# Sixteen moved tiles 96 bytes longer: where the operands of a two-layer encoder's large projections begin in memory

## The chip, the cores and the metric

The kernel runs on one core of a Trainium2 chip. The metric is the device time of one execution in microseconds (us). TensorE's clock has two levels here, 1.2 and 2.4 GHz; the trace gives the granted share of the full one.

## The reference

A trunk of two layers on 512 tokens of 1024 channels, all in float32. Each layer normalizes x, scales and shifts it by vectors that come from a condition c, projects it, mixes along the tokens, projects back, adds the result to x by a gate, and then does the same with a gated feed-forward block with a short convolution (ConvFFN, inner width 2816).

```
h = rmsnorm(x) * (1 + scale) + shift
layer 0: p = h @ ab_w_in;  y = [HGRN2 recurrence, 4 heads | RWKV-7 mixing, 8 heads](p)
layer 1: p = h @ cd_w_in;  y = [2-D Fourier mix, 4 groups | Conformer convolution](p)
x = x + gate * (y @ w_out)
u, v = split(rmsnorm(x)*(1 + scale) + shift) @ w_up)
x = x + gate * ((silu(dwconv3(u)) * v) @ w_down)
...
return rmsnorm(x) * final_g
```

## The kernel before

Activations lie with channels on the 128 partitions and the 512 tokens along the row, so x is eight tiles of 128 x 512. A projection to 128 output channels is a sum over eight input blocks in one PSUM bank. To reach float32 accuracy, each operand is split into a rounded high half and the rest (`split`, `modulate`, `load_w`), and each block costs three matmuls in `mm3` (lines 138, 139, 140): high weights by high x, high weights by low x, low weights by high x. The activations are the moved operand (512 columns); a slice of 128 x 128 weights is loaded for each matmul.

The tiles with tag "h" are that moved operand for the large input projections, the ConvFFN's up projection and the layers' output projections: 16 buffers in `hpool`, eight high and eight low halves. The same 16 buffers also serve as eight accumulators of layer 0's early output projection (`early_out`, line 867) and as the eight output tiles (line 1082). The down projection of the ConvFFN moves tiles of another pool, tag "g" (22 buffers, line 345 on); the Fourier part moves four tables of 2 x 258 columns, "tab" and "tabl" (lines 941 to 972), against weights "vh" and "vl" that come from the activations.

Memory is laid out in the order in which pools are opened, each tile rounded up to a multiple of 32 bytes a partition. First comes a scratch of 16384 bytes, then small constants, then the weight tiles (`raw` of 4096 bytes, `whi` and `wlo` of 2048), then the sixteen h tiles of 2048 bytes, then the pools of the stages. A tile "pad" of 224 bytes among the constants (line 110) makes the weight tiles begin at a multiple of 512, so the weight slices (512 bytes each), the h tiles and the g tiles all begin at multiples of 512 bytes in each partition. In the pool of layer 1, four padded inputs of 2168 bytes and the tables of 2064 bytes lie ahead of vh and vl: the four tables begin at 0, 32, 64 and 96 modulo 512 (the second half of each 8 bytes further), vh and vl at 128. The temporaries "ht" and "ot" of layer 0 begin at 416 and 288 modulo 512, the tiles "ss", "sq" and "x" at multiples of 512. The memory is full to 229152 bytes a partition.

The order of instructions on each engine comes from the framework's planner, which simulates times from the shapes of the operations and from priorities that the kernel gives (`PLAN`, `URGENT`). All transfers are issued by SyncE (SP). Weight blocks are loaded into one of three `raw` buffers, split by ScalarE (line 132) and VectorE (line 133), and then used by eight groups of three matmuls.

Of the kernel before, what the change touches and what calls it, by code (L numbers as in the profile page):

```python
# [9 lines left out]
F32 = mybir.dt.float32  # L10
F32R = mybir.dt.float32r
# [5 lines left out]
P = 128  # L17
T = 512
# [49 lines left out]
def encoder(ctx: ExitStack, tc: tile.TileContext, A, out, dbg=None):  # L68
    nc = tc.nc
    uid = [0]  # L70

    def mk(pool, shape, tag, dtype=F32, bufs=None):
        uid[0] += 1
        kw = {} if bufs is None else {"bufs": bufs}
        return pool.tile(shape, dtype, tag=tag, name=f"{tag}_{uid[0]}", **kw)
# [9 lines left out]
    hpool = ctx.enter_context(tc.tile_pool(name="hpool", bufs=16))  # L85
# [7 lines left out]
    def gps(shape=(P, T)):  # L93
        turn[0] += 1
        return mps(shape, gtags[0][turn[0] % len(gtags[0])])

    def mps(shape=(P, T), tag="m"):
        return mk(psum, list(shape), tag, bufs=banks[tag])

# [20 lines left out]
    def load_w(src, nk, pool=None, bufs=None):  # L120
        if pool is None:
            pool, bufs = spools[0]
            spools.append(spools.pop(0))
        raw = mk(wpool, [P, 8, P], "raw", bufs=3)
        nc.sync.dma_start(raw[:, :nk, :], src)
        w = []
        for k0 in range(0, nk, 4):
            n = min(4, nk - k0)
            hi = mk(pool, [P, 4, P], "whi", F32R, bufs=bufs)
            lo = mk(pool, [P, 4, P], "wlo", F32R, bufs=bufs)  # L130
            with tc.high_priority(URGENT):
                act.copy(hi[:, :n, :], raw[:, k0:k0 + n, :])  # L132
                dve.tensor_tensor(lo[:, :n, :], raw[:, k0:k0 + n, :], hi[:, :n, :].bitcast(F32), op=ALU.subtract)  # L133
            w += [(hi[:, i, :], lo[:, i, :]) for i in range(n)]
        return w
# [6 lines left out]
    def gemm(ps, w, xs, nk):  # L142
        for k in range(nk):
            mm3(ps, w[k][0], w[k][1], xs[k][0], xs[k][1], k == 0, k == nk - 1)

    def split(src):
        hi = mk(hpool, [P, T], "h", F32R)
        lo = mk(hpool, [P, T], "h", F32R)
        act.copy(hi, src)
        dve.tensor_tensor(lo, src, hi.bitcast(F32), op=ALU.subtract)  # L150
        return hi, lo

    def modulate(t, x, rs, scale, shift):

        hi = mk(hpool, [P, T], "h", F32R)
        lo = mk(hpool, [P, T], "h", F32R)
        dve.scalar_tensor_tensor(t, x, scale, rs, op0=ALU.mult, op1=ALU.mult)
        act.activation(hi, t, AF.Identity, bias=shift)  # L158
        dve.scalar_tensor_tensor(lo, t, shift, hi.bitcast(F32), op0=ALU.add, op1=ALU.subtract)  # L159
        return hi, lo  # L160
# [40 lines left out]
    def adaln(l, s, ch, tag):  # L201

        pa = mps([P, 256], tag)
        for k in range(KB):
            raw = mk(wpool, [P, 8, P], "raw", bufs=3)
            nc.sync.dma_start(raw, A["ada1"][ADA1.index((l, s, ch)), k])
            v = raw.rearrange("p g (q i) -> p q g i", q=4)
            for q in range(4):
                pe.matmul(pa[32 * q:32 * q + 32, :], sc32[:, k, :], v[:, q],
                          start=(k == 0), stop=(k == KB - 1), skip_group_check=True)  # L210
        mt = mk(const, [P, 8, 32], "mt", bufs=1)
        dve.transpose(mt.rearrange("p g i -> p (g i)"), pa)
        dve.tensor_copy(mods[l, s][0][:, ch * 8:ch * 8 + 8], mt[:, :, 0])
        finish(l, s, ch)
# [5 lines left out]
    def sc_row(pool):  # L220

        row = mk(pool, [P, D], "row")
        for i in range(2):
            ps = mps()
            for j in range(4):
                pe.matmul(ps[:, j * P:j * P + P], sc[:, 4 * i + j:4 * i + j + 1].broadcast_to([P, P]), ident,
                          start=True, stop=True)
            act.copy(row[:, i * T:i * T + T], ps)
        return row
# [31 lines left out]
    def modulated(x, mod, gsc, pool):  # L261
        rs = rstd_of(x, pool)
        hs = []
        for b in range(KB):
            t = mk(pool, [P, T], "nt", bufs=3)
            hs.append(modulate(t, x[b], rs, gsc[:, b:b + 1], mod[:, b:b + 1]))
        return hs
# [7 lines left out]
    def start_in(pool, pool2):  # L275
# [22 lines left out]
        for b in range(KB):  # L298
            raw = mk(pool, [P, 2, D], "ada", bufs=ADB)
            nc.sync.dma_start(raw, A["ada0"][b])  # L300
            if b < len(ps):
                ws[FIRST[b]] = load_w(A["ab_in"][FIRST[b]], KB, pool2, 2 * len(ps) - 2)
            with tc.high_priority(2 * URGENT):
                for i in range(2):
                    dot(raw[:, i], row, mod[:, b + 8 * i:b + 8 * i + 1])
                dve.tensor_tensor(mod[:, b:b + 9:8], mod[:, b:b + 9:8], col("ada_b", b, 9)[:, ::8], op=ALU.add)
                dve.scalar_tensor_tensor(gsc[:, b:b + 1], mod[:, 8 + b:9 + b], 1.0, col("norm_g", b), op0=ALU.add, op1=ALU.mult)
                t = mk(pool, [P, T], "nt", bufs=3)
                hs.append(modulate(t, x[b], rs, gsc[:, b:b + 1], mod[:, b:b + 1]))
# [51 lines left out]
    def layer0(ys):  # L361
# [4 lines left out]
        def lap():  # L366
            return mk(kp, [P, T], "la", bufs=4)
# [308 lines left out]
        def rwkv_post(q):  # L676
# [33 lines left out]
            if p == 3:  # L710
                late[1] = split(y)
            else:
                nc.sync.dma_start(ys[4 + p], y)
# [38 lines left out]
        def hgrn(h):  # L752
# [94 lines left out]
            if h == 3:  # L847
                late[0] = split(y)
            else:
                nc.sync.dma_start(ys[h], y)  # L850
            say(f"ya{h}", y)

        def early_out(acc, i):

            yy = []
            for k in EARLY[i]:
                y = lap()
                nc.sync.dma_start(y, ys[k])
                yy.append(split(y))
            for o in range(KB):  # L860
                if o == 4:
                    yield
                w = load_w(A["ab_out1"][i, o], len(yy))
                ps = gps()
                gemm(ps, w, yy, len(yy))
                if len(acc) == o:
                    acc.append(mk(hpool, [P, T], "h"))
                    before = lap()
                    nc.sync.dma_start(before, A["xT"][o])
                else:  # L870
                    before = acc[o]
                dve.scalar_tensor_tensor(acc[o], ps, mods[0, 0][0][:, 16 + o:17 + o], before, op0=ALU.mult, op1=ALU.add)
# [4 lines left out]
        def gate(_):  # L877
# [9 lines left out]
            "chain1": lambda p: rwkv_chain(pairs[p], units[p, 1], 1),  # L887
            "post": lambda p: rwkv_post(pairs[p]), "proj": hgrn_proj, "hgrn": hgrn, "gate": gate,
            "ada": lambda p: adaln(*ADA1[p], "g"), "out": lambda p: early_out(early, p)}
        begun, left = {}, {}  # L890

# [187 lines left out]
    for b in range(KB):  # L1079
        act.activation(x[b], x[b], AF.Copy, scale=col("final_g", b))  # L1080
    for b in range(KB):
        o = mk(hpool, [P, T], "h")
        (pl if b in (2, 5) else dve).tensor_tensor(o, x[b], rs, op=ALU.mult)
        nc.sync.dma_start(out[b], o)

# [60 lines left out]
```

## Time and profile before

| | |
|---|---|
| median of 3 runs | 1535.62 us (1531.64 to 1535.84) |
| the profiled execution | 1533.86 us, span 1532.0 us |
| TensorE busy | 1423.4 us (93%), 8114 matmuls |
| VectorE busy | 1036.5 us (68%) |
| ScalarE busy | 684.7 us (45%) |
| GpSimd busy | 160.3 us (10%) |
| mean granted TensorE clock | 0.944 |

The span runs from the first to the last instruction of the profiled execution. Layer 0 up to its output projection takes the first 615 us, its ConvFFN ends at about 985 us, layer 1's mixing at about 1150 us, and the second ConvFFN at about 1520 us; the final normalization and the stores follow. Busy matmuls overlap in the trace, since they are pipelined; the distance between their starts is what counts.

### The profile page before, as it was taken

What the parts mean: (1) busy time and instruction counts of PE and PEld (TensorE: products, weight loads), DVE (VectorE), ACT (ScalarE), POOL (GpSimd) and SP (SyncE); (2) the same over time, 40 slices, a digit from 0 to 9 for tenths busy, and PEclk for the clock granted to TensorE, in tenths of its full rate; (3) what the DMA queues carried; (4) which work ended last, traced back from release to release, by engine and by line L of the source; (5) the groups of instructions that cost most, each with busy time, mean ns of one, the idle gap of its engine ahead of it and who ended that gap; (6) DMA issues with size and microseconds to landing.
All of it is one profiled execution on the core that took longest, in us unless ns stands there. A gap on an engine that the chain in (4) does not pass through costs nothing.

```text
span 1532.0 us, 21743 instructions
## 1 busy us (share of the span) xinstructions
PE 1423.4 (93%) x8114; PEld 1108.1 (72%) x8114; DVE 1036.5 (68%) x2056; ACT 684.7 (45%) x1192; POOL 160.3 (10%) x224
## 2 busy tenths in 40 slices
PE   5988879998999998899999999898888999999996
PEld 3765666765767766688888888676756888888885
DVE  7678977697686857766566775679967653544544
ACT  4455454645544624543243243476555332332344
POOL 1030211101100000000000000069700000000000
PEclk7998888998997999999999999999899999999998
DMA  9211212332341444244544872221122332223222
GB/s 374 83 62 53 48 54 73 100 99 72 86 151 38 130 152 140 102 149 160 187 143 141 278 261 89 83 92 60 49 76 99 121 96 98 97 86 107 97 86 79
DMA packets 76282, 174.26 MB, mean 114 GB/s; under 512 B 28176, under 2 KB 33168, under 8 KB 75152
## 3 DMA queue, kind: packets, MB, share of 16 engines
q1 hardware_dynamic: 76176, 172.87, 34.3%
q8 instruction: 64, 1.05, 0.3%
q14 instruction: 42, 0.34, 0.1%
HBM read 166.02 MB, written 6.82 MB: 113 GB/s over the span
## 4 chain that ended last, share of the span: by engine, by line
PE 75%; DVE 12%; ACT 5%; DMA 3%; issue 3%; POOL 1%; SPq 0%; DVEq 0%; POOLq 0%; ACTq 0%
PE g L138 10%; PE g L139 10%; PE g L140 10%; PE c L139 6%; PE c L138 6%; PE c L140 6%; PE h L139 3%; PE h L140 3%; PE h L138 3%; PE o L139 3%; PE o L138 3%; PE o L140 3%; DVE wlo L133 2%; POOL nt L1016 1%; PE c L649 1%
## 5 line engine op out<-in xcount | busy, mean ns | idle before, releaser
L132 ACT CAST whi<-raw 128x512 fp32r<-128x512 f32 (+2 forms) x406 | 243.1, 604 | 518.6 <-PE g L139 197.3
L133 DVE TENSOR_TENSOR wlo<-raw,whi 128x512 fp32r<-128x512 f32 (+2 forms) x406 | 282.0, 699 | 183.0 <-ACT whi L132 181.9
L138 PE MATMUL g<-h,whi 128*128 128x512 f32 x620 | 255.4, 413 | 18.5 <-ACT h L158 8.0
L139 PE MATMUL g<-h,whi 128*128 128x512 f32 x620 | 251.2, 405 | 3.3 <-DVE h L159 3.3
L140 PE MATMUL g<-h,wlo 128*128 128x512 f32 x620 | 249.5, 403 | 4.8 <-DVE wlo L133 4.8
L138 PEld LDWEIGHTS g<-h,whi 128*128 128x128 f32 x620 | 120.7, 195 | 53.4 <-ACT h L158 10.9
L138 PE MATMUL c<-h,whi 128*128 128x512 f32 x334 | 133.5, 400 | 13.0 <-ACT h L158 6.0
L140 PEld LDWEIGHTS g<-h,wlo 128*128 128x128 f32 x620 | 120.3, 194 | 34.2 <-DVE wlo L133 7.7
L139 PEld LDWEIGHTS g<-h,whi 128*128 128x128 f32 x620 | 120.5, 194 | 33.7 <-DVE h L159 5.0
L140 PE MATMUL c<-h,wlo 128*128 128x512 f32 x334 | 132.9, 398 | 2.3 <-DVE wlo L133 2.3
L139 PE MATMUL c<-h,whi 128*128 128x512 f32 x334 | 133.3, 399 | 1.0 <-DVE h L159 1.0
L1016 POOL TENSOR_TENSOR nt<-nt,ta 128x512 f32<-128x512 f32 x60 | 87.6, 1472 | 3.8 <-ACT ta L1011 0.8
L138 PEld LDWEIGHTS c<-h,whi 128*128 128x128 f32 x334 | 64.5, 193 | 30.6 <-ACT h L158 7.6
L140 PEld LDWEIGHTS c<-h,wlo 128*128 128x128 f32 x334 | 64.4, 193 | 16.9 <-DVE wlo L133 3.6
L139 PEld LDWEIGHTS c<-h,whi 128*128 128x128 f32 x334 | 64.4, 193 | 15.2 <-DVE h L159 1.9
L218 DVE SCALAR_TENSOR_TENSOR ra<-ra,row 128x1024 f32<-128x1024 f32 x56 | 68.1, 1220 | 0.9 <-DMA ra<-ada 0.9
L557 DVE TENSOR_TENSOR tt<-L,xi 128x60 f32<-128x60 f32 (+24 forms) x248 | 55.9, 226 | 14.7 <-DMA L<-nd 7.7
L559 DVE TENSOR_TENSOR xi<-xi,tt 128x60 f32<-128x60 f32 (+24 forms) x248 | 53.9, 217 | 5.9
L139 PE MATMUL h<-h,whi 128*128 128x512 f32 x130 | 50.8, 391 | 0.0
L138 PE MATMUL h<-h,whi 128*128 128x512 f32 x130 | 50.8, 391 | 0.0
L140 PE MATMUL h<-h,wlo 128*128 128x512 f32 x130 | 50.8, 391 | 0.0
L138 PE MATMUL o<-h,whi 128*128 128x512 f32 x124 | 48.2, 389 | 0.0
(373 smaller groups left out, 2665.4 us busy)
## 6 DMA issues: line engine op xcount, KB each, us to landing
raw<-ffn_up SPq DMA_DIRECT2D x88, 512.0 KB, 3.3
ra<-ada SPq DMA_DIRECT2D x56, 512.0 KB, 3.7
raw<-ab_in SPq DMA_DIRECT2D x35, 512.0 KB, 3.7
raw<-ffn_down SPq DMA_DIRECT2D x32, 448.0 KB, 3.3
raw<-ada SPq DMA_DIRECT2D x24, 512.0 KB, 4.6
ada<-ada SPq DMA_DIRECT2D x8, 1024.0 KB, 10.7
raw<-ffn_down SPq DMA_DIRECT2D x16, 512.0 KB, 3.6
raw<-cd_in SPq DMA_DIRECT2D x12, 512.0 KB, 3.2
```

What stands on the lines that cost most here:

```text
L132: act.copy(hi[:, :n, :], raw[:, k0:k0 + n, :])
L133: dve.tensor_tensor(lo[:, :n, :], raw[:, k0:k0 + n, :], hi[:, :n, :].bitcast(F32), op=ALU.subtract)
L138: pe.matmul(ps, whi, xhi, start=first, stop=False)
L139: pe.matmul(ps, whi, xlo, start=False, stop=False)
L140: pe.matmul(ps, wlo, xhi, start=False, stop=last)
L218: dve.scalar_tensor_tensor(w, w, 1.0, row, op0=ALU.mult, op1=ALU.mult, accum_out=dst)
L557: dve.tensor_tensor(tv, Lv[:, j + 1:, j:j + 1].broadcast_to([P, n, m]), xi[:, j:j + 1, :m].broadcast_to([P, n, m]), op=ALU.mult)
L559: dve.tensor_tensor(xi[:, j + 1:, :m], xi[:, j + 1:, :m], tv, op=ALU.add)
L649: pe.matmul(ps[h][:, c, :], W[hr, c0 + c, :], BRS[hr, c0 + c, :], start=True, stop=True)
L1016: pl.tensor_tensor(pa, pa, tp, op=ALU.add)
```

## The change

A helper `mkh` allocates an h tile of 536 columns instead of 512 and hands out the first 512. All allocations of tag "h" go through it; the accumulators and output tiles, which were float32, are now views of the same rounded type. A tile is then 2144 bytes, so that the tile in slot i begins 96·i bytes further modulo 512 than before. To make room, the program's dynamic DMA scratch is set to 2048 bytes instead of 16384.

```diff
+    def mkh():
+
+        return mk(hpool, [P, T + 24], "h", F32R)[:, 0:T]
+
...
     def split(src):
-        hi = mk(hpool, [P, T], "h", F32R)
-        lo = mk(hpool, [P, T], "h", F32R)
+        hi = mkh()
+        lo = mkh()
...
     def modulate(t, x, rs, scale, shift):
 
-        hi = mk(hpool, [P, T], "h", F32R)
-        lo = mk(hpool, [P, T], "h", F32R)
+        hi = mkh()
+        lo = mkh()
...
-                    acc.append(mk(hpool, [P, T], "h"))
+                    acc.append(mkh().bitcast(F32))
...
-        o = mk(hpool, [P, T], "h")
+        o = mkh().bitcast(F32)
...
-    nc = bacc.Bacc("TRN2", target_bir_lowering=False, num_devices=1)
+    nc = bacc.Bacc("TRN2", target_bir_lowering=False, num_devices=1, dynamic_dma_scratch_size=2048)
```

## Rows read from the trace of the kernel before

**Rows 1.** The page: busy us (share of the span) x instructions, and clock by 40 slices

```profile
PE 1423.4 (93%) x8114; PEld 1108.1 (72%) x8114; DVE 1036.5 (68%) x2056; ACT 684.7 (45%) x1192; POOL 160.3 (10%) x224
...
PEclk7998888998997999999999999999899999999998
```

**Rows 2.** The chain that ended last, shares of the span by engine

```profile
PE 75%; DVE 12%; ACT 5%; DMA 3%; issue 3%; POOL 1%; SPq 0%; DVEq 0%; POOLq 0%; ACTq 0%
```

**Rows 3.** Windows by stage: length, busy us of each engine, granted clock, DMA

```profile
30.00:300.00 270.00, 240.26 (x1781) 176.60 (x1783) 210.44 (x527) 135.68 (x247) 39.23 (x82) 0.88 0.24 74
300.00:615.00 315.00, 291.49 (x2532) 212.10 (x2528) 237.16 (x630) 152.57 (x305) 21.64 (x48) 0.92 0.36 112
615.00:985.00 370.00, 365.42 (x1590) 299.13 (x1589) 236.51 (x375) 137.98 (x224) 0.42 (x8) 0.99 0.48 163
...
1150.00:1520.00 370.00, 365.16 (x1596) 299.97 (x1595) 191.78 (x287) 143.24 (x230) 0.00 (x0) 1.00 0.29 94
```

**Rows 4.** TensorE's groups by line and form: busy us, mean ns, idle before

```profile
L138 PE MATMUL g<-h,whi 128*128 128x512 f32 x620 | 255.4, 413 | 18.5 <-ACT h L158 8.0 <-ACT ht L729 3.5 <-ACT whi L132 2.9
...
L138 PE MATMUL c<-h,whi 128*128 128x512 f32 x334 | 133.5, 400 | 13.0 <-ACT h L158 6.0 <-ACT h L149 4.9 <-ACT whi L132 1.9
...
L138 PE MATMUL h<-h,whi 128*128 128x512 f32 x130 | 50.8, 391 | 0.0
...
L138 PE MATMUL o<-h,whi 128*128 128x512 f32 x124 | 48.2, 389 | 0.0
```

**Rows 5.** Timeline, first ConvFFN, h tiles moved: start us, us; 34 matmuls from first to last

```profile
902.49 0.39 PE L138 MATMUL c<-h,whi 128*128 128x512 f32 x1
902.49 0.19 PEld L139 LDWEIGHTS c<-h,whi 128*128 128x128 f32 x1
...
909.97 0.39 PE L138 MATMUL o<-h,whi 128*128 128x512 f32 x1
```

**Rows 6.** Timeline, second ConvFFN, g tiles moved; 34 matmuls from first to last

```profile
1506.16 0.39 PE L139 MATMUL h<-g,whi 128*128 128x512 f32 x1
...
1513.64 0.39 PE L139 MATMUL g<-g,whi 128*128 128x512 f32 x1
```

**Rows 7.** Timeline, Fourier tables moved: 9 matmuls in a row, then 8

```profile
1063.81 0.28 PE L138 MATMUL g<-tab,vh 128*128 128x258 f32 x1
...
1064.77 0.28 PE L140 MATMUL c<-tab,vl 128*128 128x258 f32 x1
...
1092.07 0.29 PE L140 MATMUL c<-tab,vl 128*128 128x258 f32 x1
...
1092.92 0.28 PE L140 MATMUL g<-tab,vl 128*128 128x258 f32 x1
```

**Rows 8.** Timeline, tables moved at the lower clock; 7 matmuls in a row

```profile
1081.13 0.42 PE L140 MATMUL c<-tab,vl 128*128 128x258 f32 x1
...
1082.42 0.42 PE L140 MATMUL g<-tab,vl 128*128 128x258 f32 x1
```

**Rows 9.** Windows of those table stretches, TensorE: length, busy, granted clock, DMA

```profile
1063.80:1064.90 1.10, 1.10 (x11) 1.00 0.00 0
...
1081.10:1082.50 1.40, 1.40 (x9) 0.50 0.00 0
1092.05:1093.00 0.95, 0.95 (x9) 1.00 0.00 0
```

**Rows 10.** VectorE's groups by form: two inputs, at multiples of 512 and at 416

```profile
L254 DVE TENSOR_TENSOR ss<-ss,sq 128x512 f32<-128x512 f32 x24 | 16.6, 691 | 2.9 <-ACT sq L250 1.3
...
L779 DVE TENSOR_TENSOR ht<-ht,ht 128x512 f32<-128x512 f32 x8 | 5.5, 684 | 0.7 <-ACT ht L777 0.7
```

**Rows 11.** DMA issues: count, KB each, median us from issue to landing

```profile
out<-h SPq DMA_DIRECT2D x8, 256.0 KB, 2.1
...
ys<-ht SPq DMA_DIRECT2D x3, 256.0 KB, 2.0
ys<-ot SPq DMA_DIRECT2D x3, 256.0 KB, 5.3
```

## The prediction

> **What bounds the kernel now.** I read the page first. TensorE is busy for 1423.4 of 1532.0 us, VectorE for 1036.5 [rows 1], and the chain that ended last runs through TensorE for 75% of the span [rows 2]. The windows by stage say where that holds [rows 3]: in the two ConvFFN stretches, 615 to 985 us and 1150 to 1520 us, TensorE is busy for 365.42 and 365.16 of 370 us at a granted clock of 0.99 and 1.00. So 740 of 1532 us are set by nothing but the distance from one matmul start to the next. In layer 0 (30 to 615 us) TensorE has gaps and the clock falls to its lower level at times (0.88 and 0.92); there some matmuls wait for other engines.
>
> Then I grouped TensorE's instructions by line and form. The tiles that the change lengthens are moved by 620 + 334 + 130 + 124 = 1208 matmuls on line 138 [rows 4], and as many on 139 and on 140: 3624 of the 8114.
>
> The timeline gives the distance. From 902.49 to 909.97 us there are 33 steps between matmuls that move h tiles: 7.48 us / 33 = 226.7 ns [rows 5]. From 1506.16 to 1513.64 us there are 33 steps between matmuls that move g tiles, which the change does not touch: again 226.7 ns [rows 6]. Both stretches run at full clock [rows 3, 9]. At the upper level, 2.4 GHz, 512 columns at one a cycle would take 213.3 ns. So each matmul takes 13.3 ns more than its columns. Whether the place where the moved tile begins has a part in these 13.3 ns is the whole question.
>
> **The change part by part.**
>
> *The place of the h tiles.* Before, the weight slices, the h tiles and the g tiles all begin at multiples of 512 bytes. After, the tile in slot i begins 96·i bytes later modulo 512; since 96·16 is 3·512, the sixteen take every multiple of 32 once, and only slot 0 stays. About 15/16 · 3624 = 3398 matmuls then read from a new place. The trace of before holds the test of this: the 258-column matmuls of the Fourier part use the same three lines and types, but their moved tables begin at 0, 32, 64 and 96 modulo 512 (the second half of each 8 bytes further), against weights at 128. Their starts lie 0.96 us over 8 steps and 0.85 us over 7 apart [rows 7], together 1.81 / 15 = 120.7 ns at full clock [rows 9]. 258 columns at 2.4 GHz are 107.5 ns: 13.2 ns over. With moved tile and weights at different places, none of them a multiple of 512 apart, the surplus is that of the 512-column matmuls that begin at the same place (13.3). At the lower level, 1.2 GHz, six steps take 1.29 us, 215 ns each [rows 8, 9], which is 258 / 1.2 and leaves no surplus. So the surplus looks like a fixed amount for each matmul at full clock, not one that hangs on the place. The two runs differ (120.0 and 121.4), so ±0.7 ns stays unknown: 3398 · 0.7 ns = 2.4 us either way. I take 0.
>
> *Slices and the extra 24 columns.* Every user gets the first 512 columns, so each instruction keeps its element count and none is added. Cost 0.
>
> *Writing and reading h on ScalarE and VectorE.* A two-input VectorE operation takes 691 ns on tiles at multiples of 512 (ss) and 684 ns on tiles at 416 modulo 512 (ht) [rows 10]. Four normalizations of eight tiles and 16 splits make 48 high and 48 low halves; with 8 accumulators and 8 output tiles 112 writes. At 7 ns apiece they are 0.8 us, in either direction, most of it behind matmuls. I take 0; without that cover it would be 0.8 us.
>
> *The output transfers.* The eight stores at the end leave h tiles that now begin at multiples of 32. A store of the same size from an h tile, at a multiple of 512, lands after 2.1 us; from an ht tile at 416 modulo 512 after 2.0 us; from an ot tile at 288, issued in busier stretches, after 5.3 us [rows 11]. Only the last landing counts: -0.1 to +3.2 us. I take 0, because the ht store is the nearest and nothing else is in the queue at the end. [...]
>
> *Everything else in the memory.* The program's dynamic DMA scratch shrinks from 16384 to 2048 bytes and all tiles move down by 14336, a multiple of 512; the pools behind the h tiles move up again by 1536, also a multiple. So no other tile changes its place modulo 512. No row shows an operation on that scratch; every transfer is issued in the program's own text on SP's queue, which the change leaves as it is. Cost 0. The planner sees the same operations with the same element counts, so I see no reason for another order of instructions.
>
> *Sum.* 1533.86 us (the profiled execution) + 0 = 1533.9 us, with -2.4 - 0.8 - 0.1 and +2.4 + 0.8 + 3.2 at the ends. The runs' median is 1535.62, 1.8 us above that execution; I forecast the median, 1535.6 us.
>
> **The rivals.**
>
> *Faster: the weight read and the moved read get in each other's way.* Each weight load starts with the matmul before it (902.49 us both, [rows 5]), and today both read from the same place modulo 512. If the whole 13.3 ns came from this, 3398 · 13.3 ns = 45.2 us would go: 1490 us. For it: all 512-column matmuls have the same surplus and the same equality of places. Against it: the tables' 13.2 ns without that equality. A part of it, up to 3 ns of the 13.3, would give -10.2 us, 1525 us. It decides from 4.6 / 3398 = 1.4 ns a matmul. [...] The chances below go by the tables.
>
> *Slower: a tile off the boundary costs one more piece.* If the 13.3 ns were four pieces of 512 bytes at 3.3 ns, a tile that begins elsewhere would touch five: 3398 · 3.3 ns = 11.2 us more, 1547 us. Decides from the same 1.4 ns. For it: the surplus has to come from somewhere. Against it: a half table of 1032 bytes touches three pieces, which would be 10 ns, and shows 13.2.
>
> *Another order.* If the planner's estimates changed after all, layer 0 would be rearranged, where TensorE is idle for 270 - 240.26 + 315 - 291.49 = 53 us [rows 3]. A tenth of that either way: 1530 or 1541 us.
>
> **How the numbers follow.** No change 0.74; the clash removed in whole 0.05 (1490) and in part 0.08 (1525); one more piece 0.10 (1547); another order 0.03, half to each side but mostly decided only beyond 4.6 us. What a measurement of this kernel tells from no change is about 0.3%, 4.6 us. Faster: 0.05 + 0.08 + 0.01 = 0.14; slower: 0.10 + 0.02 = 0.12; same 0.74. The likeliest case alone runs from 1531 to 1540 us (the ends of the sum on the median, and the runs' own spread). To hold eight in ten with cases of both signs near, the range reaches down to 1526, just short of the partial gain, and up to 1547, which takes the extra piece in.
>
> **What would show it.** After the change the same stretch of the ConvFFN should show 33 steps in 7.48 us with h tiles, and 226.7 ns with g tiles beside it; the tables 120.7 ns. If the clash is real, h steps fall towards 213.3 ns while g steps stay at 226.7, and the two ConvFFN stretches shrink by about half of the gain, since VectorE is busy for only 236.51 and 191.78 of 370 us there [rows 3] and could follow. If the extra piece is real, h steps rise to about 230 ns, and the matmuls of slot 0 stay. If layer 0 alone moves, it is the order. The prediction is wrong if the h steps move by more than 1.4 ns.

## The result and the profile after

The changed kernel is slower: 1546.74 us, the median of 4 runs (1542.96 to 1548.82), against 1535.73 us for the kernel before (4 runs, 1531.64 to 1536.39). The ratio is 1.0075, with a 95% interval from 1.0046 to 1.0104. I had forecast no change; the time lies at the upper end of the range, and the sign is that of the rival "one more piece", whose mechanism the experiments will not bear out.

The profiled execution took 1548.67 us, 14.8 us more than that of before. The page of the changed kernel, the two lines that answer to [rows 1]:

```profile
PE 1437.2 (93%) x8114; PEld 1108.1 (72%) x8114; DVE 1036.3 (67%) x2056; ACT 684.1 (44%) x1192; POOL 160.2 (10%) x224
...
PEclk7998878997996999999999999998899999999998
```

TensorE is busy for 13.8 us longer with as many matmuls; every other engine is busy for as long as before. The order of the instructions is the same on all five engines. The windows by stage, as in [rows 3]:

```profile
30.00:300.00 270.00, 237.19 (x1763) 174.41 (x1764) 209.88 (x528) 134.40 (x244) 39.12 (x81) 0.89 0.24 73
300.00:615.00 315.00, 294.94 (x2551) 213.59 (x2546) 235.86 (x629) 151.72 (x306) 21.71 (x48) 0.91 0.37 112
615.00:985.00 370.00, 363.98 (x1562) 294.65 (x1563) 233.98 (x373) 135.40 (x220) 0.00 (x0) 0.99 0.48 162
...
1150.00:1520.00 370.00, 365.81 (x1575) 296.46 (x1574) 193.11 (x289) 140.50 (x227) 0.00 (x0) 1.00 0.31 98
```

In the two ConvFFN stretches TensorE is as busy as before and the granted clock is the same 0.99 and 1.00, but the same 370 us hold 1562 and 1575 matmuls and not 1590 and 1596. So the loss is no waiting and no clock: each matmul takes longer. The timeline says which. In the first ConvFFN, the 34 matmuls that answer to [rows 5], with four of the middle:

```profile
909.06 0.39 PE L142 MATMUL c<-h,whi 128*128 128x512 f32 x1
...
912.54 0.40 PE L142 MATMUL c<-h,whi 128*128 128x512 f32 x1
912.78 0.39 PE L143 MATMUL c<-h,whi 128*128 128x512 f32 x1
913.01 0.39 PE L144 MATMUL c<-h,wlo 128*128 128x512 f32 x1
913.24 0.39 PE L142 MATMUL c<-h,whi 128*128 128x512 f32 x1
...
916.71 0.39 PE L142 MATMUL o<-h,whi 128*128 128x512 f32 x1
```

33 steps now take 7.65 us, 231.8 ns each, 5.1 ns more than in [rows 5]. The steps from 912.54 and from 913.01 belong to matmuls that move the tile in slot 0, which has not changed its place; they take 0.24 and 0.23 us like their neighbours. Over the whole trace, 220 steps without a gap at full clock that start with a tile in slot 0 take 234.8 ns on the mean, the other 3103 with h tiles 231.8. In the second ConvFFN, 33 steps with g tiles, as in [rows 6]:

```profile
1504.79 0.39 PE L144 MATMUL c<-g,wlo 128*128 128x512 f32 x1
...
1512.27 0.39 PE L144 MATMUL o<-g,wlo 128*128 128x512 f32 x1
```

7.48 us, 226.7 ns, as before. So the loss sits in the matmuls that move the lengthened tiles, and there at full clock alone. At the lower level it is absent; the timeline of layer 0, eleven steps in a row, and the window over them:

```profile
496.64 0.63 PE L143 MATMUL g<-h,whi 128*128 128x512 f32 x1
...
501.33 0.42 PE L142 MATMUL g<-h,whi 128*128 128x512 f32 x1
...
496.60:501.40 4.80, 4.80 (x13) 3.70 (x12) 3.96 (x14) 2.98 (x6) 0.00 (x0) 0.50 0.33 105
```

4.69 us / 11 = 426.4 ns at a granted clock of 0.50; in the kernel before, ten such steps from 163.69 to 167.96 us take 427.0 ns. [Rows 8, 9] have 258 columns in 215.0 ns at that clock, 0.833 ns a column; at that rate 512 columns take 426.7 ns, so nothing is on top. The prediction's 1.2 and 2.4 GHz are this rate and twice it, if a cycle moves one column; its 107.5 and 213.3 ns are then half of 215.0 and 426.7 ns, an estimate for a granted clock of 1.00. The steps at full clock and equal places in the experiments agree with it: from 320 to 512 columns they grow by (226.7 - 146.5) / 192 = 0.418 ns a column, against 0.417.

Where the time went, then: each ConvFFN's up projection has 352 matmuls with h tiles on line 142 (its groups, in that stretch), 1056 on the three lines, and 1056 · 5.1 ns = 5.4 us. The traces bear this out stage by stage, a stage being counted from its first matmul with an h tile. The first ConvFFN takes 367.9 us before and 373.4 after, the second, up to its last matmul, 361.7 and 367.4: 11.1 us together. Layer 1's mixing goes from 167.4 to 168.9. Layer 0 goes from 621.2 to 623.4, but the kernel below whose tiles are all at place 0 has 623.5 there, and the traces of the kernels below that move all 512 columns lie between 615.8 and 624.0, in no order by place; so in layer 0 nothing can be told from the spread. Of its 1032 matmuls with h tiles, 947 run wholly at full clock, so the lower clock spares few of them the price; that waits for other engines hide the rest is likely, and no run separates them.

### The profile page after: what moved, and what is told of

The parts are those of the page before. It is cut to its first block, busy times and chain, and to the rows that moved or that the text cites. A ratio compares the mean times of both kernels' runs of the same rounds, so it can differ in the third digit from the quotient of the medians.

```text
span 1546.9 us, 21743 instructions
## 1 busy us (share of the span) xinstructions
PE 1437.2 (93%) x8114; PEld 1108.1 (72%) x8114; DVE 1036.3 (67%) x2056; ACT 684.1 (44%) x1192; POOL 160.2 (10%) x224
## 4 chain that ended last, share of the span: by engine, by line
PE 75%; DVE 12%; ACT 5%; DMA 3%; issue 3%; POOL 2%; SPq 1%; DVEq 0%; POOLq 0%; ACTq 0%
PE g L142 10%; PE g L143 10%; PE g L144 10%; PE c L142 6%; PE c L143 6%; PE c L144 6%; PE h L144 3%; PE h L143 3%; PE h L142 3%; PE o L143 3%; PE o L142 3%; PE o L144 3%; DVE wlo L137 2%; POOL nt L1020 1%; PE c L653 1%
## 5 line engine op out<-in xcount | busy, mean ns | idle before, releaser
L142 PE MATMUL g<-h,whi 128*128 128x512 f32 x620 | 258.4, 418 | 19.2 <-ACT h L162 8.2
L143 PE MATMUL g<-h,whi 128*128 128x512 f32 x620 | 253.7, 409 | 3.3 <-DVE h L163 3.3
L142 PEld LDWEIGHTS g<-h,whi 128*128 128x128 f32 x620 | 121.3, 196 | 55.9 <-ACT h L162 11.1
L142 PE MATMUL c<-h,whi 128*128 128x512 f32 x334 | 136.1, 407 | 12.7 <-ACT h L162 6.0
L143 PE MATMUL c<-h,whi 128*128 128x512 f32 x334 | 135.1, 404 | 0.5 <-DVE h L163 0.5
```

The costliest lines, as they stand in the source:

```text
L142: pe.matmul(ps, whi, xhi, start=first, stop=False)
L143: pe.matmul(ps, whi, xlo, start=False, stop=False)
```

## The experiments

Eleven kernels ran, in four groups. Each is the kernel before with another layout, and two also move fewer columns; where nothing else is said, `mkh`, the smaller scratch and the views are those of the change. "Place" is where a tile begins, modulo 512 bytes; the weight slices are at place 0 unless said otherwise.

**1. Place, sequence or length.** Is it the longer tiles and the new layout as such, the changing places from one matmul to the next, or the places themselves? The first kernel has longer tiles still, all at place 0:

```diff
-        return mk(hpool, [P, T + 24], "h", F32R)[:, 0:T]
+        return mk(hpool, [P, T + 128], "h", F32R)[:, 0:T]
```

> The h tiles are 512 bytes longer each (2560 bytes) and the scratch is 2048 bytes, so all sixteen begin at a multiple of 512 again, in memory that is otherwise shifted as after the change. Theory place (a moved tile that begins off a multiple of 512 costs an extra piece): h steps 226.7 ns, the time of before. Theory sequence (what costs is that a matmul's moved tile begins elsewhere modulo 512 than the one before it): 226.7 ns, the time of before. Theory layout (longer tiles, smaller scratch or the shifted pools cost): h steps near 232 ns, about 11 us over before.

It took 1533.89 us against 1531.96, ratio 1.0010 [0.9989, 1.0032]. The timeline of it, 33 steps with h tiles in the first ConvFFN:

```profile
903.83 0.39 PE L144 MATMUL g<-h,wlo 128*128 128x512 f32 x1
...
911.31 0.39 PE L143 MATMUL o<-h,whi 128*128 128x512 f32 x1
```

7.48 us, 226.7 ns. Length, scratch and layout cost nothing that shows. The second kernel keeps the old stride, so that all sixteen tiles are at one and the same place, 96:

```diff
+    before_h = ctx.enter_context(tc.tile_pool(name="before_h", bufs=1))
     hpool = ctx.enter_context(tc.tile_pool(name="hpool", bufs=16))
+    after_h = ctx.enter_context(tc.tile_pool(name="after_h", bufs=1))
...
-        return mk(hpool, [P, T + 24], "h", F32R)[:, 0:T]
+        return mk(hpool, [P, T], "h", F32R)[:, 0:T]
...
+    mk(before_h, [P, 24], "before_h")
+    mk(after_h, [P, 104], "after_h")
```

> The h tiles have their old length, and all sixteen begin at 96 modulo 512; weight slices stay at 0. Theory place: every moved tile is off the boundary, so h steps of 232 ns or more and 11 us or more over before. Theory sequence: all moved tiles begin at the same place, so 226.7 ns and the time of before. A third theory, relation (the moved tile begins elsewhere than the weight slice): 232 ns, about 11 us over before.

1550.39 us, ratio 1.0107 [1.0075, 1.0139]: slower than the change itself. The timeline of this kernel, 33 steps with h tiles in the first ConvFFN, then 33 with g tiles (place 0) in the second:

```profile
904.98 0.40 PE L147 MATMUL c<-h,whi 128*128 128x512 f32 x1
...
912.69 0.39 PE L146 MATMUL c<-h,whi 128*128 128x512 f32 x1
...
1504.82 0.39 PE L147 MATMUL g<-g,whi 128*128 128x512 f32 x1
...
1512.30 0.39 PE L147 MATMUL o<-g,whi 128*128 128x512 f32 x1
```

7.71 us / 33 = 233.6 ns against 226.7 ns. Since no place changes from one h matmul to the next here, the sequence is not the cause. At the lower clock this kernel pays nothing either: 64 steps with h tiles there take 426.8 ns on the mean.

**2. Which places.** The same edit with other lengths: `T + 64`, whose places are 0 and 256, and `T + 32`, whose places are 0, 128, 256 and 384.

> Each h tile is 256 bytes longer, so that the tiles begin at 0 and 256 modulo 512 in turn; high and low half of a block mostly lie at different ones. Theory place: half of the matmuls pay, h steps 229 to 230 ns on the mean, 5 us over before. Theory sequence: two of three steps change the place; 226.7 ns only for the others, and 5 to 11 us over before, unless places 256 apart are the same to the chip (then the time of before).

> Each h tile is 128 bytes longer; the tiles begin at 0, 128, 256 and 384 modulo 512. Theory place: three quarters of the matmuls pay, h steps near 231 ns, 8 us over before. Theory sequence: nearly every step changes the place, h steps near 232 ns, 11 us over before, unless places 128 apart are the same to the chip (then the time of before).

`T + 64` took 1532.31 us, ratio 1.0003 [0.9983, 1.0023]. The timeline of it, 33 steps in the first ConvFFN:

```profile
903.63 0.39 PE L144 MATMUL g<-h,wlo 128*128 128x512 f32 x1
...
911.11 0.39 PE L143 MATMUL o<-h,whi 128*128 128x512 f32 x1
```

7.48 us, 226.7 ns: tiles at 256 are as good as at 0, also mixed. `T + 32` took 1543.47 us, ratio 1.0064 [1.0039, 1.0088]. The timeline of it, 48 steps in the first ConvFFN:

```profile
904.67 0.40 PE L143 MATMUL c<-h,whi 128*128 128x512 f32 x1
...
915.74 0.40 PE L143 MATMUL g<-h,whi 128*128 128x512 f32 x1
```

11.07 us / 48 = 230.6 ns. So places 256 bytes apart count as the same, and places 128 apart do not.

**3. Place, or relation to the weights?** This kernel moves the weights as well: they and all h tiles are at 96, the g tiles stay at 0.

```diff
+    after_h = ctx.enter_context(tc.tile_pool(name="after_h", bufs=1))
...
-        return mk(hpool, [P, T + 24], "h", F32R)[:, 0:T]
+        return mk(hpool, [P, T], "h", F32R)[:, 0:T]
...
+    mk(after_h, [P, 104], "after_h")
...
-    mk(const, [P, 56], "pad")
+    mk(const, [P, 80], "pad")
```

> Weight tiles and h tiles both begin at 96 modulo 512, the g tiles stay at 0. Theory place (a moved tile off a multiple of 256 bytes costs, whatever the weights do): h steps 233 ns as with h alone at 96, g steps 226.7 ns, about 16 us over before. Theory relation (moved tile and weight slice must begin at the same place modulo 256): h steps 226.7 ns, and g steps, 1056 of them, near 233 ns, about 6 us over before. If weights off the boundary cost by themselves, both h and g steps are above 226.7.

The timeline of it, h tiles in the first ConvFFN and g tiles in the second:

```profile
904.75 0.39 PE L145 MATMUL c<-h,whi 128*128 128x512 f32 x1
...
912.23 0.39 PE L145 MATMUL o<-h,whi 128*128 128x512 f32 x1
...
1504.73 0.39 PE L146 MATMUL g<-g,wlo 128*128 128x512 f32 x1
...
1512.46 0.40 PE L146 MATMUL h<-g,wlo 128*128 128x512 f32 x1
```

The h matmuls, at 96 against weights at 96, are back at 7.48 us / 33 = 226.7 ns; the g matmuls, at place 0 and in the second kernel free, now take 7.73 / 33 = 234.2 ns. Nothing was done to the g tiles. What costs is the difference between the place of the moved tile and that of the weight slices, not either by itself. The same kernel has a control of its own: 144 matmuls at its start take their weights from another pool (`startw`), which stays at 0, and 122 of their steps, h tiles at 96 against weights at 0, take 233.3 ns on the mean, though the `raw` blocks lie at 96 for them too. The whole took 1541.61 us against 1534.49, ratio 1.0048 [1.0031, 1.0064]: 7.1 us, where 1056 g matmuls at 7.5 ns make 7.9.

Two more kernels give each stage a place of its own, so that further differences show in the timelines: 32 in layer 0, 64 and 128 for h and g in the first ConvFFN, 160 in layer 1, 192 and 224 in the second ConvFFN; and in the other kernel 96, 16 and 8, 4, 112 and 48. Is there one that is better than 0? The edit of the first of the two, in columns of 4 bytes:

```diff
+    place = [8]
...
-        return mk(hpool, [P, T + 24], "h", F32R)[:, 0:T]
+        return mk(hpool, [P, T + 128], "h", F32R)[:, place[0]:place[0] + T]
...
+        place[0], gplace = ((16, 32), (48, 56))[l]
```

> One place for each stage, with tiles of 2560 bytes and a shifted view: h at 32 bytes in layer 0, 64 in the first ConvFFN, 160 in layer 1, 192 in the second; g at 128 and 224. Theory place: 226.7 ns nowhere, since none is a multiple of 256; 230 to 234 ns in each, more or less alike. If only multiples of 64 (or 128) count, the stages at 64 and 192 (or 128) show 226.7.

> The same with other places: h at 96 bytes in layer 0, 16 in the first ConvFFN, 4 in layer 1, 112 in the second; g at 8 and 48. Theory place: all above 226.7 ns, as soon as the tile is one element off; if the cost grows with the distance from the boundary, 4 and 8 cost least.

They took 1548.83 and 1547.04 us (a run of each), beside 1534.49 for the kernel before. Each mean is of 33 steps in a row at full clock, those at 0, 96 and 256 from the kernels above:

| difference, bytes | 0, 256 | 4 | 8 | 16 | 32 | 48 | 64 | 96 | 112 | 128 | 160 | 192 | 224 |
|---|---|---|---|---|---|---|---|---|---|---|---|---|---|
| ns a step | 226.7 | 236.7 | 233.3 | 231.8 | 233.3 | 233.6 | 228.8 | 233.6 | 231.2 | 232.4 | 234.2 | 233.3 | 233.3 |

The timeline rows of the dearest, layer 1 of the second of these kernels, 4 bytes off:

```profile
1004.82 0.40 PE L146 MATMUL g<-h,wlo 128*128 128x512 f32 x1
...
1012.63 0.40 PE L145 MATMUL g<-h,whi 128*128 128x512 f32 x1
```

7.81 us / 33 = 236.7 ns. So the cost does not grow with the distance, by which 4 and 8 would have been the cheapest. The g tiles of the kernel with weights at 96 are 160 apart from them modulo 256 (0 - 96), and their 234.2 ns is that of the h tiles at 160 against weights at 0: that is as it should be if the difference modulo 256 alone counts. None of the twelve differences beats 0; others were not tried. 226.7 ns is the least that any of the kernels shows over 33 such steps of 512 columns.

**4. Why the tables misled.** The prediction's test was the 258-column matmuls. This kernel is the kernel before, without `mkh`, and gives the tables' halves multiples of 512 bytes and so the same place as vh and vl:

```diff
-            hi = mk(lp, [P, 2, H + 2], f"tab{i}", F32R)
-            lo = mk(lp, [P, 2, H + 2], f"tabl{i}", F32R)
+            hi = mk(lp, [P, 2, H + 128], f"tab{i}", F32R)[:, :, 0:H + 2]
+            lo = mk(lp, [P, 2, H + 128], f"tabl{i}", F32R)[:, :, 0:H + 2]
```

> The kernel before, with each half of the four Fourier tables at a multiple of 512 and their weights vh and vl too. If the tables paid for their places all along (my prediction took their 120.7 ns as proof that places cost nothing), their step falls below 120.7 ns, to 115 or so. If 120.7 ns is what 258 columns cost anyway, it stays. The total stays within its spread either way, since only 48 matmuls change.

1531.51 us, a single run. The timeline of it, eight steps with tables moved at full clock:

```profile
1061.46 0.28 PE L138 MATMUL g<-tab,vh 128*128 128x258 f32 x1
...
1062.42 0.28 PE L140 MATMUL c<-tab,vl 128*128 128x258 f32 x1
```

0.96 us / 8 = 120.0 ns; with a second run of seven (1089.76 to 1090.59 us, 0.83 us) it is 1.79 / 15 = 119.3 ns, against 120.7 in [rows 7]. Equal places bring at most 1.4 ns at 258 columns. Two kernels then vary the length in the ConvFFN itself, at place 0 and at place 96. They leave out a part of the sums: only the first input block of each moves all columns.

```diff
-    def gemm(ps, w, xs, nk):
+    def gemm(ps, w, xs, nk, n=T):
         for k in range(nk):
-            mm3(ps, w[k][0], w[k][1], xs[k][0], xs[k][1], k == 0, k == nk - 1)
+            m = T if k == 0 else n
+            mm3(ps[:, 0:m], w[k][0], w[k][1], xs[k][0][:, 0:m], xs[k][1][:, 0:m], k == 0, k == nk - 1)
...
-                    gemm(pu, wu, hs, KB)
+                    gemm(pu, wu, hs, KB, (258, 384)[l])
...
-                    gemm(ps, w, gs, nj)
+                    gemm(ps, w, gs, nj, (320, 448)[l])
```

> All moved tiles of the large projections begin at multiples of 512 bytes, as the weights do. Left out: in the ConvFFN's projections only the first input block moves all 512 columns; the other blocks move 258 (first up projection), 320 (first down), 384 (second up) and 448 (second down) columns, so the last tokens miss those blocks' part. Control for the next kernel: it gives the step at equal places for each length. Expected by the row for 258-column tables: 120 to 121 ns at full clock; if the surplus over one column a cycle is a fixed 13.3 ns: 146.6, 173.3 and 200.0 ns for 320, 384 and 448 columns; if it grows with the columns (13.3 for 512): 8.3, 10.0 and 11.6 ns over, so 114.2 at 258, 141.6, 170.0 and 198.3.

> The same lengths, and the same part left out, with the moved tiles at 96 modulo 512 against weights at 0. Theory fixed (what unequal places cost is one amount for each matmul, whatever its length): all four lengths show 6 to 7 ns more than at equal places, and the 258-column tables of the kernel before, which show 0 to 1 ns, need another reason. Theory columns (the cost comes as the columns are read, and more than in proportion): about 0 to 1 ns at 258 columns, 2 to 5 at 384, 5 to 6 at 448, 6.7 at 512; in proportion it would be 3.4, 4.2, 5.0 and 5.9 ns.

They took 1362.86 and 1369.89 us (a run of each): 7.0 us between two kernels that differ in the place alone. The timeline with 384 columns in the second ConvFFN: at place 0, twelve steps,

```profile
1192.11 0.33 PE L142 MATMUL c<-h,whi 128*128 128x384 f32 x1
...
1194.19 0.33 PE L142 MATMUL c<-h,whi 128*128 128x384 f32 x1
```

and at place 96, fifteen steps:

```profile
1192.25 0.34 PE L142 MATMUL g<-h,whi 128*128 128x384 f32 x1
...
1194.90 0.34 PE L142 MATMUL g<-h,whi 128*128 128x384 f32 x1
```

2.08 / 12 = 173.3 ns and 2.65 / 15 = 176.7 ns. For the other lengths, 20 steps in a row of each (512 from the kernels above):

| columns | at 0.417 ns a column (estimate) | equal places | 96 bytes apart | cost of the difference |
|---|---|---|---|---|
| 258 | 107.5 | 119.5 | 120.0 | 0.5 |
| 320 | 133.3 | 146.5 | 146.5 | 0.0 |
| 384 | 160.0 | 173.3 | 176.7 | 3.4 |
| 448 | 186.7 | 202.5 | 205.5 | 3.0 |
| 512 | 213.3 | 226.7 | 233.6 | 6.9 |

(The starts are given to 10 ns, so 20 steps are good to some 0.5 ns.) Over every step of each length at full clock, more than 400 of each in either kernel, the means are 120.2 and 120.3 ns at 258 columns, 146.5 and 146.8 at 320, 174.4 and 176.6 at 384, and 203.0 and 205.3 at 448: the difference costs 0.1, 0.4, 2.2 and 2.3 ns. So up to 320 columns it costs next to nothing; beyond, it does. The fixed theory falls. The theory of the columns holds in its form, but 448 columns show less than the 5 to 6 ns that it gave. There and, by the means over all steps, at 384 the matmuls at equal places already take more than a surplus of 13.3 would give (200.0 and 173.3), so equal places are not free at every length.

The last kernel puts only the low halves at 96, so that of the three matmuls of a block only the second moves from an unequal place:

```diff
-    def mkh():
+    def mkh(o=0):
 
-        return mk(hpool, [P, T + 24], "h", F32R)[:, 0:T]
+        return mk(hpool, [P, T + 128], "h", F32R)[:, o:o + T]
...
     def split(src):
         hi = mkh()
-        lo = mkh()
+        lo = mkh(24)
...
     def modulate(t, x, rs, scale, shift):
 
         hi = mkh()
-        lo = mkh()
+        lo = mkh(24)
```

> High halves of the moved tiles begin at multiples of 512, low halves at 96 modulo 512, weights at multiples of 512: of the three matmuls of each block only the second moves from an unequal place. Theory own step: the step that starts with that matmul rises by 6 to 8 ns, the two others stay at 226.7; mean of three 228.7 to 229.4. Theory carried: the price falls on the step after or before it, or on all three; if each matmul pays for the relation of its own columns to the weights that are being loaded for the next one, the step after which a changed place follows is the one that rises. Whole time, in both: a third of what all at 96 cost, 1536 + 5 = 1541 us.

1541.11 us, a single run, beside 1535.17 for the kernel before. The timeline of it, 33 steps, eleven blocks of three, in the first ConvFFN:

```profile
904.73 0.40 PE L142 MATMUL c<-h,whi 128*128 128x512 f32 x1
...
912.36 0.40 PE L142 MATMUL o<-h,whi 128*128 128x512 f32 x1
```

7.63 us / 33 = 231.2 ns, above the 228.7 to 229.4 that I expected. One matmul in three off its place costs 4.5 ns on the mean of the three, 13.5 ns a block, twice the 6.9 that a matmul costs where all are off. From the trace's starts, over some 800 blocks of both up projections and layer 1, the step from the first matmul to the second is 233.3 ns, from the second to the third 230.9, from the third to the next block's first 229.4. So the price is carried: matmuls at an equal place pay for a neighbour that is not. That fits slot 0, which pays after the change among neighbours that are off. The whole time of 1541 us came as expected, but by luck: the two ConvFFN stages are 4.8 and 5.2 us longer than before, where all tiles at 96 cost 6.7 in each, and layer 0 was 3.7 us shorter in this execution.

## Why the prediction was wrong, point by point

**What bounds the kernel: right.** The matmuls with h tiles set the time of the ConvFFN stretches, and 5.1 ns on each went through to the end there: the windows show TensorE full in both, and the two stages are 5.4 and 5.7 us longer. That layer 0 has room in its gaps held too: its 1032 matmuls with h tiles left nothing in the whole that stands out.

**The place of the h tiles: wrong, and the whole miss.** The step that failed is "So the surplus looks like a fixed amount for each matmul at full clock, not one that hangs on the place", and the 0 (± 2.4 us) taken from it. The observation was sound: 258-column matmuls with unequal places do show 13.2 ns over their columns, and they show no more than 1.4 ns less with equal ones. What failed was to carry it to 512 columns. The lengths show that the cost of unequal places is 0.1 ns at 258 columns, 0.4 at 320 and 6.9 at 512, so the tables could not have shown it. In its place: the 13.3 ns are what is left when the places are equal modulo 256 bytes, and unequal places add to them, 5.1 ns a matmul in the mix of the change. 3624 · 5.1 ns = 18.5 us is the term if every matmul counted; the two ConvFFN stages show 11.1 of it, layer 1 at most 1.5 and layer 0 nothing that stands out, and the medians differ by 11.0. That a price had been bounded only at half the length of the matmuls in question was visible in the rows, and the bound of ±0.7 ns left it out. The range of the likeliest case has a slip of its own: the ends of the sum (-3.3 and +6.4 us) on the median of 1535.6 give 1532 to 1542 us; 1531 to 1540 are those on the profiled execution.

**The rival "faster": the right pair, with the sign the wrong way round.** It named the weight read and the moved read as what might get in each other's way, and took equality of places for the clash. The kernel with weights at 96 shows that the pair matters and that equality is the case without the cost: 226.7 ns at equal places and 233.6 at 96 apart, for the same matmuls.

**The rival "one more piece": the right time by luck, another mechanism.** It gave 1547 us and steps of about 230 ns, and 1546.74 us and 231.8 ns came. But its 1547 us came from 3.3 ns on 3398 matmuls, where 5.1 ns on the 2112 of the ConvFFNs make nearly the same; it let slot 0 stay, and slot 0 pays; and it charged a tile for not beginning on a boundary, while tiles at 96 against weights at 96 cost nothing (226.7 ns), and g tiles on the boundary cost 7.5 ns there.

**The other terms: right at 0, but for the stores.** The kernel with tiles of 2560 bytes has the longer tiles, the views and the smaller scratch, and a ratio of 1.0010. The order of instructions stayed as it was. For writing the halves, the groups on ScalarE and VectorE that write most of them, two rows before and two after:

```profile
L158 ACT ACTIVATE h<-nt,mod 128x512 fp32r<-128x512 f32 x32 | 22.6, 724 | 32.4 <-DVE nt L157 32.4
L159 DVE SCALAR_TENSOR_TENSOR h<-nt,mod,h 128x512 fp32r<-128x512 f32 x32 | 23.4, 749 | 0.5
...
L162 ACT ACTIVATE h<-nt,mod 128x512 fp32r<-128x512 f32 x32 | 22.6, 724 | 31.5 <-DVE nt L161 31.5
L163 DVE SCALAR_TENSOR_TENSOR h<-nt,mod,h 128x512 fp32r<-128x512 f32 x32 | 23.3, 745 | 0.5
```

724 ns both times and 745 against 749: nothing is lost by the new places. The stores are the exception. Their times from issue to landing, first before and then after:

```profile
DMA to landing us min/median/max: 2.0/2.1/2.5
...
DMA to landing us min/median/max: 2.0/2.2/2.7
```

The longest is the last store's, and it goes from 2.5 to 2.7 us. The traces of all thirteen kernels agree: it is 2.52 to 2.54 us in the six whose output tiles all begin at multiples of 256 bytes, 2.71 to 2.74 in the six where most or all do not, and 2.56 in `T + 32`, where half do not. So this term is 0.2 us and not 0, inside its bounds of -0.1 to +3.2, and the 2.0 us of the ht store did not stand for it.

**What stays open.** What makes the 13.3 ns at equal places, and why 4 bytes apart cost most and 64 least, no run shows. That two reads of the same memory meet is my inference from the relation, the carrying over and the absence of any cost at the lower clock (426.8 ns with all tiles at 96), and no run shows it; whether it is a matmul's own weights or those being loaded for the next one was not separated. Why 448 columns show only 2 to 3 ns, and why equal places are not free there, is open too.

## What to carry to other kernels

Where TensorE streams 512-column matmuls like these (rounded float32, a weight load for each) at full clock, let the moved tiles and the weight slices begin at the same place modulo 256 bytes: against 96 apart that was worth 3% of each such step here (6.9 of 233.6 ns), and the twelve differences that were tried gave away 1 to 4% (2.1 to 10.0 ns). Look at the step from start to start by tile, since busy shares and clock show nothing of it. And a null result on a shorter instruction bounds only the shorter instruction: before a price of 0 is carried over, ask whether the cost could begin between the two lengths.

## What the hardware showed that I had not expected

The step of a matmul hangs on the relation of two addresses: 226.7 ns at 0 or 256 bytes apart, 228.8 to 236.7 at twelve other distances. The cost is not confined to the matmul with the odd place: one in three off costs 13.5 ns a block. It is there at 384 and 448 columns (2.2 and 2.3 ns) and at 512 (6.9), hardly at 258 and 320 (0.1 and 0.4), and it is gone at the lower clock (426.4 ns, and 426.8 with all tiles at 96). The last of the eight stores landed 0.2 us later from tiles off a multiple of 256 bytes (2.7 us against 2.5).
